# A hybrid diffusion layer: the prompt's 24 projection tiles interleaved with halves of two of the sample's tiles, in a PSUM layout of their own

## The chip, the cores and the metric

The kernel runs on one core of a Trainium2 chip. TensorE (PE) multiplies, VectorE (DVE), ScalarE (ACT) and GpSimd (POOL) compute beside it, and SyncE (SP) issues most of the transfers between the chip's memory and SBUF; TensorE writes to PSUM, of which there are 8 banks of 512 float32 columns. The metric is the device time of one execution in microseconds (us); lower is better. Each engine works through its own queue in order, and waits on semaphores for the others.

## The reference, cut to what matters

One layer is computed for two groups of tokens that share all weights: a prompt of 256 tokens and a sample of 1024 tokens, both with 1024 channels.

```python
mod = silu(c) @ w_ada + b_ada                       # six modulation vectors per group
h   = rmsnorm(x, g_norm1) * (1 + scale_m) + shift_m
proj = h @ w_in                                     # 1024 -> 3*512 + 512 + 1024 + 2*8
hc, gb, gc, z, xbc, dtf, dtb = split(proj)
out_a = gb * dwconv1d(gc * hc, w_conv_short)        # "outa"
xbc   = silu(dwconv1d(xbc, w_conv_ssd, b_conv_ssd)) # X, B, C of the scan
dt_f, dt_b = softplus(dtf + dt_bias[0]), softplus(dtb + dt_bias[1])
y   = ssd_scan(...) + reversed ssd_scan(...) + xh * d_skip
y   = rmsnorm(y * silu(z), g_ssd_norm)
x   = x + gate_m * (concat([out_a, y]) @ w_out)
...                                                 # gated ConvFFN: w_up, convolution, w_down
```

All of it is float32. The projection `h @ w_in` is the work in which the change lies, together with the cumulative sums of `dt` that the scan needs and with the modulation vectors of the FFN.

## The kernel before

**A float32 product in three.** Each operand is split into a high part (type fp32r) and the rest, and a product is made of three matmuls, hi·hi, hi·lo and lo·hi (`mm3`, L160, L162 and L164). `h` is split once. A weight tile, 128 output channels by 1024 inputs, is split when it is loaded (`wload`): a DMA brings 512 KB into a raw buffer, ACT copies it to `whi` (L151), and DVE or POOL subtracts to get `wlo` (L77; the last argument of the tile functions, `PV` or `PG`, says which). There are two buffers each of `whi` and `wlo`, and every third tile takes the single `whx`/`wlx` instead, so three split tiles can exist at a time. The raw buffers of the prompt's tiles have the tag `x` (8 of them), those of the sample's tiles the tag `raw` (2, one of which holds the sample's raw `dt` rows until `dtstage(SS)` has read them).

**Tiles of `w_in`.** Each group has 24: four each for `hc`, `gb`, `gc` and `z`, and eight for `xbc`. A tile of the prompt is 24 matmuls of 256 columns (`acc<-bc` in the rows), one of the sample 48 of 512 columns (`acc<-h`). Functions do one tile with what follows it: `xbc` (bias, convolution along the tokens; L396 is its ACT copy out of PSUM), `zproj` (copy at L409, written out by L410), and `outa` (three tiles: `hc` copied at L423, scaled at L431, `gc` multiplied into it, `gb` multiplied in, the result written out at L443 and L444 and read back by L872 for `w_out`).

**The order of the program around the change.**
1. Modulation blocks for the first norm, and beside them the sample's `xbc` tiles 0 and 1, in one loop over the inputs (L332, `N_LOOP` = 2).
2. The prompt's 24 tiles: eight `xbc`, four `zproj`, four `outa`. In between `dtstage(SP)` and `dttok(SP)`: a chain of some 20 small operations on DVE and ACT that turns the prompt's `dt` rows into decays (L458 on PE starts it; L461 to L502), and transposes of its results on PE (L513, and L523 with what L520 makes).
3. `dtstage(SS)`, the same chain for the sample; then the sample's `xbc` tiles 2 to 6, each followed by `ada(2)` to `ada(5)` in two steps: one of the four modulation vectors left, 32 small matmuls (L177) on 8 buffers `x` of `w_ada`, and transposes (L189) behind the next tile. `dttok(SS)` comes in the fifth of them, after tiles 2, 3 and 4.
4. The scan of both groups, with the sample's `z`, seventh `xbc` and `outa` tiles as fillers, and then `w_out` (L160 to L164 with `acc<-ya` and `acc<-oa`) and the FFN.

**Who sets the order.** Within this program order a list scheduler puts each engine's instructions in a row by their estimated times, and pools give out buffers: a tile with a tag waits until the buffer's last reader is done. PSUM up to `w_out` is one pool with `acc` (2 buffers of 2 banks), `yp` (1 bank) and `sa` (3 banks). When one pool is closed and another opened in its place, SBUF pools wait tile by tile (`reuse_waits="tile"`), PSUM pools for all of what the old pool held:

```python
def open_pool(name, side="left", **kw):
    if "space" not in kw:
        kw["reuse_waits"] = "tile"
```

Of the kernel before, what the change touches and what calls it, by code (L numbers as in the profile page):

```python
# [10 lines left out]
PSUM = bass.MemoryType.PSUM  # L11
DRAM = bass.MemoryType.DRAM

P = 128
# [19 lines left out]
N_LOOP = 2  # L34
# [21 lines left out]
def body(nc, tc, A):  # L56
    cnt = [0]

    def T(pool, shape, tag, bufs, dt=F32):
        cnt[0] += 1  # L60
        return pool.tile(list(shape), dt, tag=tag, bufs=bufs, name=f"{tag}_{cnt[0]}")

    def open_pool(name, side="left", **kw):
        if "space" not in kw:
            kw["reuse_waits"] = "tile"
        g = tc.tile_pool(name=name, bufs=1, side=side, **kw)
        return g, g.__enter__()

    def close_pool(g):
        g.__exit__(None, None, None)  # L70
# [8 lines left out]
    def stt(out, a, s, b, op0, op1):  # L79
        V.scalar_tensor_tensor(out=out, in0=a, scalar=s, in1=b, op0=op0, op1=op1)  # L80
# [14 lines left out]
    def smv(n):  # L95
        a, b = SMO[n]
        return sm[:, a:b]
# [25 lines left out]
    g_nrm, nrm = open_pool("nrm")  # L123
    wx = [nrm]
    g_ps, ps = open_pool("ps1", space=PSUM)

    def pacc():
        return T(ps, [P, 1024], "acc", 2)

    def pst():  # L130
        return T(ps, [P, 512], "yp", 1)
# [1 line left out]
    def psa():  # L133
        return T(ps, [P, 512], "sa", 3)
# [175 lines left out]
    for k in range(KT):  # L310
# [7 lines left out]
        x = xs[k]  # L318
# [15 lines left out]
        q, i = k // 4, k % 4  # L334
# [11 lines left out]
    for name, t0, n, v in (("p", 0, TP, 0), ("s", TP, TS, 1)):  # L346
        s = S()
# [5 lines left out]
    SP, SS = sets  # L353
# [5 lines left out]
    def proj(s, m, lo_eng):  # L359
        g = proj_halves(s, m, lo_eng)  # L360
        next(g)
        return next(g)

    def proj_halves(s, m, lo_eng):
        s.n += 1
        wh, wl = wload(A["w_in"][m], lo_eng, T(nrm, [P, KT, P], "x", 8) if s.name == "p" else None)
        pp = psa() if s.name == "p" and s.n <= 2 else pacc()
        outs = []
        for a, b in s.chunks:
            outs.append((pp[:, a:b], (lambda k, a=a, b=b: s.hi(k)[:, a:b]),  # L370
                         (lambda k, a=a, b=b: s.lo(k)[:, a:b])))
        ks = list(range(KT))
        for half in (ks[0:KT // 2], ks[KT // 2:]):
            ends = mm3(outs, wh, wl, KT, half)
            mid_mm[0] = ends[0]
            last_mm.append(ends[-1])
            yield pp[:, 0:s.T]

    def conv1d_sb(out, u, w, n):
        stt(out[:, 1:n], u[:, 0:n - 1], w[0], out[:, 1:n], ALU.mult, ALU.add)  # L380
        stt(out[:, 0:n - 1], u[:, 1:n], w[2], out[:, 0:n - 1], ALU.mult, ALU.add)

    def xbc(s, i, out, lo_eng):
        w = [smv("wcx")[:, i * 3 + t:i * 3 + t + 1] for t in range(3)]
        b = smv("bcx")[:, i:i + 1]
        if s.name == "s" and i < N_LOOP:
            u = pps[i]
            for c in range(2):
                act(out[:, c * 512:(c + 1) * 512], u[c], AF.Identity, scale=w[1], bias=b)
            stt(out[:, 1:513], u[0], w[0], out[:, 1:513], ALU.mult, ALU.add)  # L390
            stt(out[:, 513:TS], u[1][:, 0:511], w[0], out[:, 513:TS], ALU.mult, ALU.add)
            stt(out[:, 0:511], u[0][:, 1:512], w[2], out[:, 0:511], ALU.mult, ALU.add)
            stt(out[:, 511:TS - 1], u[1], w[2], out[:, 511:TS - 1], ALU.mult, ALU.add)
        else:
            pp = proj(s, 16 + i, lo_eng)
            act(out, pp, AF.Identity, scale=w[1], bias=b)  # L396
            conv1d_sb(out, pp, w, s.T)

    def zproj(s, j, lo_eng):
        for _ in zproj_halves(s, j, lo_eng):  # L400
            pass
# [45 lines left out]
    def dtcopy(s, pd):  # L447
        d4 = T(wst, [P, s.T], "raw", 2) if s.name == "s" else T(cv, [P, s.T], "cv", 4)
        for a, b in s.chunks:
            act(d4[:, a:b], pd[a // 512][:, 0:b - a], AF.Copy)  # L450
        return d4
# [53 lines left out]
    def dttok(s, v, e2, ce):  # L505
        s.tok = T(sd, [P, s.nc, 2, 40], f"tok{s.name}", 1)
        for c0 in range(0, s.nc, 4):
            cn = min(4, s.nc - c0)
            tp = psa()
            for c in range(cn):  # L510
                for i, src in enumerate((v, e2)):
                    o = (c * 2 + i) * 40
                    mm = nc.tensor.transpose(tp[:, o:o + 40], src[:, (c0 + c) * L:(c0 + c + 1) * L],  # L513
                                             ident[0:40, 0:40])
                    if c0 == c == i == 0:
                        after(mm, last_mm[-1])
            act(s.tok[:, c0:c0 + cn].rearrange("p c i r -> p (c i r)"), tp[:, 0:cn * 80], AF.Copy)
        dg = T(cv, [40, 8, 40], "cv", 4)
        for i in range(s.nc):
            V.tensor_scalar(out=dg[:, i, :], in0=ident[0:40, 0:40], scalar1=ce[:, i:i + 1],  # L520
                            scalar2=None, op0=ALU.mult)
        pdx = psa()
        nc.tensor.matmul(pdx[:, 0:s.nc * 40], ones[0:40, :],  # L523
                         dg[:, 0:s.nc].rearrange("p c r -> p (c r)"), start=True, stop=True)
        s.dec = T(sd, [P, s.nc, 40], f"dec{s.name}", 1)
        s.last_exp = act(s.dec.rearrange("p c r -> p (c r)"), pdx[:, 0:s.nc * 40], AF.Exp)
# [161 lines left out]
    PV, PG = nc.vector, nc.gpsimd  # L688
# [11 lines left out]
    for i in range(N_LOOP):  # L700
        xbc(SS, i, SS.X[i], PG)
        act(SS.X[i], SS.X[i], AF.Silu)
    for i in range(8):
        xbc(SP, i, (SP.X + bcp)[i], PG if i % 3 else PV)
        if i == 5:
            pd_p = [psa()]
            dtmm(pd_p, range(KT), lambda k: xp[k // 4][:, k % 4], TP)
            d4_p = dtcopy(SP, pd_p)
    act(xall, xall, AF.Silu)
    silu = act(bcall, bcall, AF.Silu)  # L710
    for j in range(4):
        zproj(SP, j, PG if j % 2 else PV)
        if j == 0:
            dts = dtstage(SP, d4_p, silu)
    for j in range(4):
        for _ in outa(SP, j, PG):
            pass
        if j == 0:
            dttok(SP, *dts)
    dts = dtstage(SS, d4_s, silu)  # L720


    bcs = [T(sd, [P, TS], "bc", 4) for _ in range(4)]
# [3 lines left out]
    def silu_s(i):  # L727
        after(act(xbcs[i], xbcs[i], AF.Silu), SS.last_exp)

    pend = None  # L730
    for i in range(N_LOOP, 7):
        xbc(SS, i, xbcs[i], PV)
        if pend is not None:
            next(pend)
            pend = None
        if i == 4:
            dttok(SS, *dts)
            for k in range(N_LOOP, 4):
                silu_s(k)
        if i >= 4:  # L740
            silu_s(i)
        if i < 6:
            pend = ada(i, lambda: T(nrm, [P, 1024], "x", 8))
            next(pend)
    make_aff(1, 4, "g2")
    wx[0] = None
# [116 lines left out]
    g_ps, ps = open_pool("ps2", space=PSUM)  # L863
# [382 lines left out]
```

## Time and profile before

| what | us |
|---|---|
| median of three runs | 1574.92 |
| lowest and highest of them | 1574.71 and 1576.44 |
| the profiled execution | 1575.34 |
| its span in the trace | 1573.4 |
| PE busy (8722 matmuls) | 1522.2, 97% |
| DVE, ACT and POOL busy | 1104.6, 662.1 and 514.6 |

The mean granted TensorE clock in the profiled execution was 0.993. PE is the engine to read: the time that it waits, and the time in which its clock is low, are what an order of work can save here. A row of the timeline gives the start in the span, the duration, the engine, the line, what is written and read, and in brackets how long the engine had been idle before and what it waited for; in groups, xN is the number of instructions. A row's duration on PE covers a matmul from its start to its modelled end, so matmuls in a row overlap; the step from start to start is what one costs.

### The profile page before, as it was taken

The page shows a single profiled execution, that of the slowest core. Times are in us where ns is not written, and L with a number is a line of the kernel's source. Part 1 is how long each engine was busy: PE and PEld are TensorE (multiplying, and loading weights), DVE is VectorE, ACT ScalarE, POOL GpSimd, SP SyncE. Part 2 cuts the span into 40 slices and gives each one's busy share as a digit, 9 for nine tenths or more (in the row PEclk, how much of TensorE's full clock was granted, in tenths as well). Part 3 has the DMA queues.
Part 4 walks back from the last instruction along what each step waited for, and adds up shares of the span by engine and source line. Part 5 has one row for each costly group of instructions (what it writes and reads, how often), then busy time and mean ns, then how long its engine had stood idle before and what let it go on. Part 6 is the DMA issues. An engine that isn't in the chain of part 4 may idle for free. (4 is left out here: it accounts for less than half of the span.)

```text
span 1573.4 us, 22518 instructions
## 1 busy us (share of the span) xinstructions
PE 1522.2 (97%) x8722; PEld 1296.7 (82%) x8722; DVE 1104.6 (70%) x1634; ACT 662.1 (42%) x1025; POOL 514.6 (33%) x288
## 2 busy tenths in 40 slices
PE   6989999999999999999999999999999999999997
PEld 3688667778787888888888888898888888888886
DVE  5765615367887349796666598656679878798696
ACT  6553334257777135433322253322334433433333
POOL 1445001111120001344333333333346545455452
PEclk9999999999999999999999999999999999999999
DMA  8555554343434712222222242222252333343221
GB/s 305 215 185 167 211 203 147 110 151 132 139 116 142 287 54 102 93 74 68 69 77 74 66 143 96 73 66 67 88 173 96 97 108 95 101 161 98 94 77 61
DMA packets 86908, 191.98 MB, mean 122 GB/s; under 512 B 9330, under 2 KB 36626, under 8 KB 86802
## 3 DMA queue, kind: packets, MB, share of 16 engines
q1 hardware_dynamic: 80978, 187.41, 35.1%
q10 hardware_dynamic: 5824, 3.15, 0.7%
q8 instruction: 68, 1.11, 0.3%
q14 instruction: 38, 0.31, 0.1%
HBM read 167.37 MB, written 23.15 MB: 121 GB/s over the span
## 5 line engine op out<-in xcount | busy, mean ns | idle before, releaser
L80 DVE SCALAR_TENSOR_TENSOR cc<-acc,sm,cc 128x504 f32<-128x504 f32 (+5 forms) x836 | 545.9, 665 | 110.2 <-ACT cc L986 51.9
L77 POOL TENSOR_TENSOR wlo<-raw,whi 128x1024 fp32r<-128x1024 f32 (+2 forms) x83 | 194.0, 2337 | 666.7 <-ACT whi L151 541.6
L151 ACT ACTIVATE whi<-raw 128x1024 fp32r<-128x1024 f32 x90 | 95.1, 1057 | 240.9 <-PE acc L162 218.0
L80 DVE SCALAR_TENSOR_TENSOR x<-dn,mod,x 128x288 f32<-128x288 f32 (+2 forms) x176 | 96.1, 547 | 95.1 <-PE dn L164 94.4
L77 POOL TENSOR_TENSOR dlo<-draw,dhi 128x512 fp32r<-128x512 f32 (+1 forms) x88 | 109.0, 1239 | 90.2 <-ACT dhi L1039 88.2
L160 PE MATMUL acc<-ya,whi 128*128 128x512 f32 (+1 forms) x400 | 119.4, 356 | 3.4 <-DVE cv L77 3.4
L164 PE MATMUL acc<-ya,wlo 128*128 128x512 f32 (+1 forms) x400 | 119.5, 356 | 0.0
L162 PE MATMUL acc<-ya,whi 128*128 128x512 f32 (+1 forms) x400 | 119.5, 356 | 0.0
L164 PE MATMUL acc<-oa,wlo 128*128 128x512 f32 (+1 forms) x400 | 118.9, 355 | 0.0
L162 PE MATMUL acc<-oa,whi 128*128 128x512 f32 (+1 forms) x400 | 118.7, 354 | 0.0
L160 PE MATMUL acc<-oa,whi 128*128 128x512 f32 (+1 forms) x400 | 118.2, 353 | 0.0
L160 PE MATMUL dn<-yb,dhi 128*128 128x288 f32 (+2 forms) x352 | 110.0, 313 | 5.3 <-DVE x L80 4.1
L77 POOL TENSOR_TENSOR wlx<-raw,whx 128x1024 fp32r<-128x1024 f32 (+2 forms) x32 | 74.0, 2313 | 119.2 <-ACT whx L151 104.5
L162 PE MATMUL dn<-yb,dhi 128*128 128x288 f32 (+2 forms) x352 | 109.6, 311 | 0.8 <-POOL yb L77 0.8
L164 PE MATMUL dn<-yb,dlo 128*128 128x288 f32 (+2 forms) x352 | 109.5, 311 | 0.0
L160 PE MATMUL acc<-h,whi 128*128 128x512 f32 x320 | 104.1, 404 | 0.0
L1039 ACT ACTIVATE dhi<-draw 128x512 fp32r<-128x512 f32 (+1 forms) x88 | 53.0, 602 | 121.4 <-PE dn L162 50.0
L162 PE MATMUL acc<-h,whi 128*128 128x512 f32 x320 | 101.0, 395 | 0.0
L164 PE MATMUL acc<-h,wlo 128*128 128x512 f32 x320 | 100.1, 394 | 0.0
L160 PE MATMUL dn<-g,dhi 128*128 128x288 f32 (+2 forms) x304 | 95.1, 313 | 0.0
L162 PE MATMUL dn<-g,dhi 128*128 128x288 f32 (+2 forms) x304 | 94.7, 312 | 0.3 <-POOL g L77 0.3
L164 PE MATMUL dn<-g,dlo 128*128 128x288 f32 (+2 forms) x304 | 94.7, 312 | 0.0
(340 smaller groups left out, 3631.8 us busy)
## 6 DMA issues: line engine op xcount, KB each, us to landing
raw<-in_w_up SPq DMA_DIRECT2D x88, 512.0 KB, 3.2
x<-in_w_ada SPq DMA_DIRECT2D x32, 512.0 KB, 5.4
draw<-in_w_down SPq DMA_DIRECT2D x64, 256.0 KB, 2.7
x<-in_w_in SPq DMA_DIRECT2D x24, 512.0 KB, 3.3
raw<-in_w_in SPq DMA_DIRECT2D x22, 512.0 KB, 4.3
xs<-in_w_ad SPq DMA_DIRECT2D x16, 512.0 KB, 8.4
csb<-csds SPq DMA_DIRECT2D x16, 512.0 KB, 3.9
raw<-in_w_out SPq DMA_DIRECT2D x16, 512.0 KB, 3.2
```

Of the source, the lines that this page charges most:

```text
L77: (eng or V).tensor_tensor(out=out, in0=a, in1=b, op=op)
L80: V.scalar_tensor_tensor(out=out, in0=a, scalar=s, in1=b, op0=op0, op1=op1)
L151: act(hi, raw, AF.Copy)
L160: nc.tensor.matmul(o, wh[:, k, :], rh(k), start=k == 0, stop=False)
L162: nc.tensor.matmul(o, wh[:, k, :], rl(k), start=False, stop=False)
L164: mm = nc.tensor.matmul(o, wl[:, k, :], rh(k), start=False, stop=k == n - 1)
L1039: act(wh, raw, AF.Copy)
```

## The change

The prompt's part (stage 2) gets a PSUM layout of its own. The first pool is closed after the loop of stage 1. A second has `pj` (three buffers of one bank) for the prompt's tiles, `sa` as before, and a single `acc` of two banks; a third, opened after `dtstage(SS)`, has the layout of before. PSUM pools now also wait tile by tile, here and at `w_out`.

In the prompt's part two of the sample's tiles are done, each in two halves of four inputs (`xbc_halves`): tile 2 after the prompt's `xbc` 3 and 7, tile 3 after the last `zproj` and after the second `outa`. The split weights of such a tile stay in their buffers from the first half to the second. `ada(2)` follows the second `outa` and is finished after the third; the first step of `ada(3)` follows the fourth. The loop of stage 3 begins with tile 4, so that one tile of the sample instead of three lies between `dtstage(SS)` and `dttok(SS)`.

```diff
     def open_pool(name, side="left", **kw):
-        if "space" not in kw:
+        if kw.get("space") != DRAM:
             kw["reuse_waits"] = "tile"
...
     def pacc():
-        return T(ps, [P, 1024], "acc", 2)
+        return T(ps, [P, 1024], "acc", 1 if ph_p[0] else 2)
+    ph_p = [False]
+    def pj():
+        return T(ps, [P, 512], "pj", 3)
...
-        pp = psa() if s.name == "p" and s.n <= 2 else pacc()
+        pp = pj() if s.name == "p" else pacc()
...
     def xbc(s, i, out, lo_eng):
+        for _ in xbc_halves(s, i, out, lo_eng):
+            pass
+    def xbc_halves(s, i, out, lo_eng):
...
-            pp = proj(s, 16 + i, lo_eng)
+            g = proj_halves(s, 16 + i, lo_eng)
+            next(g)
+            yield
+            pp = next(g)
             act(out, pp, AF.Identity, scale=w[1], bias=b)
             conv1d_sb(out, pp, w, s.T)
+            yield
...
+    close_pool(g_ps)
+    g_ps, ps = open_pool("ps2", space=PSUM)
+    ph_p[0] = True
+    def ada_s(cc):
+        return ada(cc, lambda: T(nrm, [P, 1024], "x", 8))
+    xs_g = [xbc_halves(SS, i, SS.X[i], PV) for i in (2, 3)]
     for i in range(8):
         xbc(SP, i, (SP.X + bcp)[i], PG if i % 3 else PV)
...
+        if i in (3, 7):
+            next(xs_g[0])
...
     for j in range(4):
         zproj(SP, j, PG if j % 2 else PV)
         if j == 0:
             dts = dtstage(SP, d4_p, silu)
+    next(xs_g[1])
     for j in range(4):
         for _ in outa(SP, j, PG):
             pass
         if j == 0:
             dttok(SP, *dts)
+        if j == 1:
+            next(xs_g[1])
+            pend = ada_s(2)
+            next(pend)
+        if j == 2:
+            next(pend)
+    pend = ada_s(3)
+    next(pend)
     dts = dtstage(SS, d4_s, silu)
+    close_pool(g_ps)
+    g_ps, ps = open_pool("ps3", space=PSUM)
+    ph_p[0] = False
...
-    for i in range(N_LOOP, 7):
+    for i in range(4, 7):
         xbc(SS, i, xbcs[i], PV)
         if pend is not None:
             next(pend)
...
         if i == 4:
             dttok(SS, *dts)
             for k in range(N_LOOP, 4):
                 silu_s(k)
-        if i >= 4:
-            silu_s(i)
+        silu_s(i)
         if i < 6:
-            pend = ada(i, lambda: T(nrm, [P, 1024], "x", 8))
+            pend = ada_s(i)
             next(pend)
```

Lines below the first edit move down by 5, 13 or more: L160, L162 and L164 become L165, L167 and L169; L177 becomes L182, L396 L408, L409 L422, L458 L471, L493 L506, L513 L526, and L523 L536. Three places show how instructions stand. The names end in a running number; `pj_...` and `acc_...` are PSUM accumulators, `whi_...`, `whx_...` and so on split weights, `x_...` raw buffers.

ACT at the prompt's last `z` tiles, before. L472 and L493 belong to `dtstage(SP)`, and each L409 frees the accumulator of a `z` tile.

```order
L472 ACTIVATE cv_160_912<-cv_161_914 40x256 [waits DVE_49,Activation_49]
L409 ACTIVATE xl_172_1004<-acc_171_979 128x256 [waits DMAHW5_49,PE_49]
L151 ACTIVATE whi_184_1076<-x_183_1074 128x1024
L410 DMA zd_114_565<-xl_172_1004 128x2x128 [waits DMAHW0_49,Activation_49]
L151 ACTIVATE whi_189_1112<-x_188_1110 128x1024 [waits DMAHW7_49,PE_49,Pool_49]
L493 ACTIVATE cv_157_904<-cv_157_904 40x256 [waits DVE_49]
L409 ACTIVATE xl_177_1038<-acc_176_1013 128x256 [waits DMAHW6_49,PE_49]
```

The same place with the change:

```order
L485 ACTIVATE cv_164_974<-cv_165_976 40x256 [waits DVE_49,Activation_49]
L156 ACTIVATE whi_187_1136<-x_186_1134 128x1024 [waits DMAHW6_49,PE_49]
L422 ACTIVATE xl_176_1066<-pj_175_1041 128x256 [waits DMAHW5_49,PE_49]
L423 DMA zd_114_565<-xl_176_1066 128x2x128 [waits DMAHW1_49,Activation_49]
L506 ACTIVATE cv_161_966<-cv_161_966 40x256 [waits DVE_49]
L156 ACTIVATE whx_192_1169<-x_191_1167 128x1024 [waits PE_49,Pool_49]
L515 ACTIVATE cv_163_971<-cv_163_971 40x256 [waits DVE_49]
L422 ACTIVATE xl_181_1100<-pj_180_1075 128x256 [waits DMAHW7_49,PE_49]
```

The last `z` tile's accumulator still comes free behind L506 (L493 before) and now behind two more instructions; but `pj` has three buffers, and PE has the first half of the sample's tile 3 ahead of the tile that takes that buffer again.

SP before, at the loads of the prompt's last two `outa` tiles (`x<-in_w_in`) and the first of `ada(2)` (`x<-in_w_ada`):

```order
L149 DMA x_231_1376<-in_w_in 128x1024 [waits DMAHW6_49,DMAHW1_49,Pool_49]
L490 DMA csdp_109_560<-cv_161_914 4x2x128 [waits DMAHW3_49,DVE_49]
L490 DMA csdp_109_560<-cv_161_914 4x2x128 [waits DMAHW4_49]
L490 DMA csdp_109_560<-cv_161_914 4x2x128 [waits DMAHW5_49,DVE_49]
L490 DMA csdp_109_560<-cv_161_914 4x2x128 [waits DMAHW6_49]
L149 DMA x_236_1409<-in_w_in 128x1024 [waits DMAHW7_49,Pool_49]
L149 DMA x_241_1445<-in_w_in 128x1024 [waits DMAHW0_49,Pool_49]
L174 DMA x_264_1585<-in_w_ada 128x1024 [waits DMAHW1_49,Pool_49]
```

SP with the change, where the last loads of `ada(2)` and the first for the third `outa` stand:

```order
L179 DMA x_232_1410<-in_w_ada 128x1024 [waits DMAHW6_49,Pool_49]
L456 DMA oad_113_564<-xl_221_1356 128x256 [waits DMAHW7_49,Activation_49]
L457 DMA oad_113_564<-xl_222_1358 128x256 [waits DMAHW0_49,DVE_49]
L154 DMA x_235_1427<-in_w_in 128x1024 [waits DMAHW1_49,PE_49]
L154 DMA x_240_1460<-in_w_in 128x1024 [waits DMAHW2_49,PE_49]
L154 DMA x_245_1496<-in_w_in 128x1024 [waits DMAHW6_49,DMAHW3_49,PE_49]
```

And PE with the change, from the middle of the first step of `ada(2)` to the first `outa` tile behind it:

```order
L182 MATMUL sa_224_1390<-x_226_1392,sc_7_77 32x512
L182 MATMUL sa_224_1390<-x_225_1391,sc_7_77 32x512
L182 MATMUL sa_223_1389<-x_232_1410,sc_7_77 32x512 [waits DMAHW6_49]
L182 MATMUL sa_223_1389<-x_231_1409,sc_7_77 32x512 [waits DMAHW5_49]
L182 MATMUL sa_223_1389<-x_230_1408,sc_7_77 32x512 [waits DMAHW2_49]
L182 MATMUL sa_223_1389<-x_229_1407,sc_7_77 32x512 [waits DMAHW1_49]
L182 MATMUL sa_224_1390<-x_232_1410,sc_7_77 32x512
L182 MATMUL sa_224_1390<-x_231_1409,sc_7_77 32x512
L182 MATMUL sa_224_1390<-x_230_1408,sc_7_77 32x512
L182 MATMUL sa_224_1390<-x_229_1407,sc_7_77 32x512
L165 MATMUL pj_238_1433<-bc_36_173,whi_236_1429 128x256 [waits Activation_49]
L167 MATMUL pj_238_1433<-bc_38_175,whi_236_1429 128x256
```

Before, the loads of the `outa` tiles waited for POOL, the last reader of an earlier prompt tile, and those of `ada(2)` came behind them. Now the eight buffers `x` are with `ada(2)` when the third `outa` asks for three, and the load of `x_235_1427` waits for PE, for the row of L182 that reads `x_226_1392` last (the first of the rows above); the weights made of it, `whi_236_1429`, are what the tile `pj_238_1433` reads.

PE at `dttok(SS)`, before: `acc_277_1627` and `acc_295_1737` are the sample's tiles 3 and 4, with `acc_261_1531`, tile 2, ahead of them. L458 starts `dtstage(SS)` ahead of all three.

```order
L458 MATMUL sa_248_1484<-raw_117_568,cst_2_66 40x512
L458 MATMUL sa_249_1487<-raw_117_568,cst_2_66 40x512 [waits PE_49]
L160 MATMUL acc_261_1531<-h_52_225,whx_259_1527 128x512 [waits DVE_49]
...
L164 MATMUL acc_295_1737<-h_107_532,wlo_294_1734 128x512 x2
L189 MATMUL sa_296_1789<-cst_2_66,x_290_1727 128x128 [waits DVE_49,Activation_49]
L189 MATMUL sa_296_1789<-cst_2_66,x_290_1727 128x128 x3
L189 MATMUL sa_297_1796<-cst_2_66,x_291_1729 128x128 [waits Activation_49]
L189 MATMUL sa_297_1796<-cst_2_66,x_291_1729 128x128 x3
L513 MATMUL sa_299_1804<-cst_2_66,cv_247_1483 128x40 [waits PE_49]
```

With the change (`acc_295_1745` is tile 4, `acc_319_1892` tile 5):

```order
L471 MATMUL sa_282_1694<-raw_117_568,cst_2_66 40x512 [waits DVE_49]
L471 MATMUL sa_283_1697<-raw_117_568,cst_2_66 40x512 [waits Activation_49]
L165 MATMUL acc_295_1745<-h_52_225,whi_293_1741 128x512 [waits DVE_49]
...
L169 MATMUL acc_295_1745<-h_107_532,wlo_294_1742 128x512 x2
L194 MATMUL sa_296_1797<-cst_2_66,x_279_1689 128x128 x4
...
L165 MATMUL acc_319_1892<-h_78_362,whx_317_1888 128x512 x2
L526 MATMUL sa_299_1812<-cst_2_66,cv_281_1693 128x40 [waits DVE_49,PE_49]
L167 MATMUL acc_319_1892<-h_79_365,whx_317_1888 128x512 x2
```

Between the start of the chain (L458, now L471) and the first instruction that needs its end (L513, now L526) stood three tiles of the sample; now there are one tile and 20 matmuls of the next.

More of the change, by code (lines that the diff above doesn't have):

```diff
@@ L728, in silu_s @@
         after(act(xbcs[i], xbcs[i], AF.Silu), SS.last_exp)
-    pend = None
-    for i in range(N_LOOP, 7):
+    for i in range(4, 7):
         xbc(SS, i, xbcs[i], PV)
```

## The prediction

> **What bounds the kernel now.** I read the page's first part, then PE's waits, then the stretch of the prompt's tiles by windows and the timeline, and last the place where the PSUM pool changes at `w_out`.
>
> ```profile
> PE 1522.2 (97%) x8722; PEld 1296.7 (82%) x8722; DVE 1104.6 (70%) x1634; ACT 662.1 (42%) x1025; POOL 514.6 (33%) x288
> ```
>
> PE is busy for all but 51 us of the span, and the change neither adds nor removes a matmul. So it can only move the idle time and the clock of PE. PE's waits, in all, times, longest:
>
> ```profile
> PE yp L243 <- DVE cv L77: 11.0, 1, 11.0
> ...
> PE acc L160 <- DVE cv L77: 3.4, 1, 3.4
> ...
> PE sa L523 <- DVE cv L520: 3.4, 1, 3.4
> ...
> PE acc L160 <- ACT xl L409: 3.3, 1, 3.3
> ...
> PE acc L160 <- ACT bcp L396: 1.0, 1, 1.0
> ```
>
> The 11.0 us are the start of the kernel, untouched. The other four are where the change works: the first at `w_out`, the rest in the prompt's part. There the windows show busy time by engine, then the clock:
>
> ```profile
> core 0: us, PE busy (x) PEld busy (x) DVE busy (x) ACT busy (x) POOL busy (x), PEclk, DMA share, GB/s
> 110.00:120.00 10.00, 6.67 (x51) 6.47 (x50) 8.28 (x14) 3.05 (x6) 4.99 (x2) 0.93 0.44 145
> 120.00:130.00 10.00, 6.58 (x43) 6.21 (x43) 6.32 (x7) 3.58 (x8) 7.11 (x3) 0.84 0.40 137
> 130.00:140.00 10.00, 10.00 (x77) 10.00 (x76) 2.37 (x2) 3.36 (x5) 4.70 (x2) 0.89 0.42 124
> ```
>
> and PE's rows show that an idle of 3.3 or 3.4 us costs twice:
>
> ```profile
> 113.71 0.28 PE L162 MATMUL acc<-bc,whx 128*128 128x256 f32 x1
> 113.83 0.28 PE L164 MATMUL acc<-bc,wlx 128*128 128x256 f32 x1
> 117.44 0.39 PE L160 MATMUL acc<-bc,whi 128*128 128x256 f32 x1 [3.33 <-ACT xl L409]
> ...
> 118.61 0.41 PE L160 MATMUL acc<-bc,whi 128*128 128x256 f32 x1
> 118.81 0.42 PE L162 MATMUL acc<-bc,whi 128*128 128x256 f32 x1
> ...
> 121.81 0.38 PE L160 MATMUL acc<-bc,whi 128*128 128x256 f32 x1
> ...
> 128.74 0.58 PE L523 MATMUL sa<-cv,ones 40*128 40x80 f32 x2 [3.42 <-DVE cv L520]
> ```
>
> A prompt matmul steps by 0.12 us (113.71 to 113.83), but 15 of them, from 118.61 to 121.81, take 3.2 us, 0.213 each: 15 × 0.093 = 1.4 us lost to the clock. The idle ahead of 128.74 is followed by as much: the window from 130 has PE at 10.00 busy with a clock of 0.89, 11% of 10 us or 1.1, and some of it falls before 130; I take 1.4 again. The part now loses 1.0 + 3.3 + 3.4 + 2.8 = 10.5 us.
>
> The reason for the 3.3 us: ACT frees the accumulator, and stood in `dtstage(SP)`.
>
> ```profile
> 116.71 0.42 ACT L493 ACTIVATE cv<-cv 40x256 f32<-40x256 f32 x1 [4.44 <-DVE cv L492]
> 117.03 0.36 ACT L409 ACTIVATE xl<-acc 128x256 f32<-128x256 f32 x1
> ```
>
> **What goes.** L409 (now L422) still stands behind that chain, but the tile that takes the bank again is now the third behind it, with a half of a sample tile ahead. Half a tile is 12 pairs of 512 columns at 0.46 us, 5.5 us, and two tiles of the prompt are 2 × 24 × 0.12 = 5.8:
>
> ```profile
> 168.24 0.62 PE L160 MATMUL acc<-h,whx 128*128 128x512 f32 x2
> 168.70 0.62 PE L162 MATMUL acc<-h,whx 128*128 128x512 f32 x2
> ```
>
> 11.3 us of cover for an evacuation that was 3.3 late: that wait and its 1.4 of clock go. The 1.0 behind the `xbc` tiles goes with the third bank. Without this cover they would come back in full, 4.7 us. Two steps cost nothing: SP passes the `ada` loads ahead of the last `outa` loads, and the first `ada` loads go out while PE runs tiles whose weights are in already; the added PSUM pools issue no instruction, and the wait at their border is for tiles that were read some tiles ago.
>
> **What comes.** Prices of the steps of a weight tile, and of what stands between them:
>
> ```profile
> 102.91 2.40 POOL L77 TENSOR_TENSOR wlo<-x,whi 128x1024 fp32r<-128x1024 f32 x1 [3.34 <-ACT whi L151]
> 92.01 1.06 ACT L151 ACTIVATE whi<-x 128x1024 fp32r<-128x1024 f32 x1 [2.06 <-PE acc L162]
> 78.54 2.01 ACT L702 ACTIVATE xs<-xs 128x1024 f32<-128x1024 f32 x2
> 80.45 0.55 ACT L396 ACTIVATE xp<-sa,sm 128x256 f32<-128x256 f32 x1
> 79.23 1.22 DVE L77 TENSOR_TENSOR wlx<-x,whx 128x1024 fp32r<-128x1024 f32 x1
> 87.80 0.99 DVE L80 SCALAR_TENSOR_TENSOR xp<-acc,sm,xp 128x255 f32<-128x255 f32 x2
> 81.11 0.28 PE L160 MATMUL acc<-bc,whx 128*128 128x256 f32 x1
> 169.72 3.64 PE L177 MATMUL sa<-x,sc 128*32 128x512 f32 x32
> ```
>
> 1. *The fourth prompt tile.* The first three now share three banks, and the first bank's evacuation stands behind the two silus of the sample's tiles on ACT and `wlx` on DVE. PE gets there at 81.1, as before, since the same work is ahead. The silus end at 80.5, `whx` at 81.5, `wlx` on DVE at 82.7, the two convolution steps at 83.7: 2.5 us late by these rows. The silus wait for the loop's last matmuls, which now have no prompt rows between them and come a little sooner; I take 1.8, ends 1.0 and 2.6.
> 2. *Three sets of weights.* The sample's tile keeps its set between its halves, so two are left for the prompt, and a tile's set is the one that the tile before it has just left. From its release it takes 1.06 + 2.40, and 0.1 to 0.3 of passing on: 3.6 to 3.75 us. PE has other work, counted in its row of instructions, of 2.1 us at the eighth `xbc` tile, 3.1 at the third tile of `outa` 0 and 2.5 at that of `outa` 1. Waits of 1.5, 0.5 and 1.2; ends 0.8 and 2.0 for the first, 0 and 1.8 for the others.
> 3. *`dttok(SP)`*: L536 (L523 before) waits for the same two DVE steps behind the same convolution. PE comes later by what terms 1 and 2 cost, which the chain partly shares. I take 2.0 of the 3.4; ends 1.0 and 3.4.
> 4. *The third `outa`.* The load of its first weights now waits for the 14th of the 32 matmuls of `ada(2)`: 14/32 × 3.64 = 1.6 us into them. Then DMA, ACT and POOL follow one another, and PE has nothing in its row but the rest of `ada(2)` and two matmuls. The loads, from issue to landing:
>
> ```profile
> x<-in_w_in SPq DMA_DIRECT2D x24, 512.0 KB, 3.3
> x<-in_w_ada SPq DMA_DIRECT2D x32, 512.0 KB, 5.4
> ```
>
> 1.6 + 3.3 + 1.1 + 2.4 + 0.2 of passing on = 8.6, against 3.64 + 0.24 = 3.9 of PE: a wait of about 4.8. If the transfer takes 5.4, as in the bursts of `ada`, it is 6.9; with one at 2.0 us, 3.5. I take 3.3, as it is the first of its burst. Behind it POOL's 2.4 per tile keeps up with PE's 2.9.
> 5. *`dttok(SS)`.* The sample's chain, from its first ACT step to its last product on DVE:
>
> ```profile
> 160.50 1.24 ACT L461 ACTIVATE cv<-sa,rows 40x512 f32<-40x512 f32 x2
> ...
> 180.99 1.20 DVE L77 TENSOR_TENSOR cv<-cv,cv 40x1024 f32<-40x1024 f32 x1
> ```
>
> 182.2 − 160.5 = 21.7 us, of which two weight steps of DVE in its middle, 2 × 1.2, now stand elsewhere: 19.3. Before, three tiles of 11 us and two steps of `ada` covered it. Now one tile (11.0), eight transposes (an estimate of 1.0) and 20 matmuls (4.6) do, 16.6 us: a wait of 2.7, and 0.3 for the later ones of the same chain, 3.0; ends 1.5 and 5.
> 6. *The clock.* Waits 4 and 5 are as long as those that cost 1.4 us each: one surely, the other as likely as not to be long enough in one piece, 1.4 + 1.0 = 2.4; ends 1.4 and 3.5.
>
> The Trainium skill ("TensorE: Matmul & The Clock Gate", Part 1, "What's actually happening") states that the array's clock is halved after an idle window of about 3.4 us, stays so for about as long a busy one, and that the window runs free. The 3.2 us of slow steps behind an idle of 3.33 agree. By that rule wait 5 costs either nothing or a full window, an estimate of 0 or 1.7 us, which would make the sum 1579.1 or 1580.8. It speaks against turning several short waits into one long one.
>
> Together 1.8 + 3.2 + 2.0 + 4.8 + 3.0 + 2.4 = 17.2 us, against 10.5: +6.7.
>
> **At `w_out`** the first accumulator waits for all of the old pool, the last `outa` tile's DVE step among it, and the clock falls.
>
> ```profile
> 508.32 1.22 DVE L77 TENSOR_TENSOR cv<-acc,cv 128x1024 f32<-128x1024 f32 x1
> 509.69 0.59 PE L160 MATMUL acc<-ya,whi 128*128 128x256 f32 x2 [3.39 <-DVE cv L77]
> ...
> 515.51 0.51 PE L160 MATMUL acc<-oa,whi 128*128 128x256 f32 x2
> 515.86 0.51 PE L162 MATMUL acc<-oa,whi 128*128 128x256 f32 x2
> ...
> 522.21 0.51 PE L162 MATMUL acc<-oa,whi 128*128 128x256 f32 x2
> 513.86 3.14 SPq L872 DMA_DIRECT2D oa<-oad  x2
> oa<-oad SPq DMA_DIRECT2D x2, 384.0 KB, 3.7
> ```
>
> Tile by tile it takes the banks of the tile before the last and could start at 506.3: 3.4 us and the clock's 1.6 sooner (a pair steps by 0.35 us, so that the 12 pairs before 515.51 are worth 4.2; they took 5.8), 5.0 in all. But two loads that it reads late, `oa`, are issued at 513.9 and 516.7 whatever PE does, since they follow the last `outa` tile out to memory and back. They land at 517.6 and 520.4. Row 522.21 needs the second; now it can run at 520.4. So 1.8 of the 5.0 is left, ends 0 and 5.0. Late next is the second `oa` load, instead of DVE.
>
> **The sum.** +6.7 − 1.8 = +4.9, on 1575.3 for the profiled execution (0.4 above the median): 1580 us.
>
> **The rivals.**
> - *The halves do cover the preparation (faster).* ACT, DVE and POOL would be a tile or more ahead behind each 5.5 us half, so that terms 1, 2 and 4 vanish with one clock loss: 1.8 + 3.2 + 4.8 + 1.4 = 11.2 off, 1569. It turns on one thing, whether a weight set and a buffer `x` come free 3.5 us (for `x`, 7 us) ahead of use. For it speaks POOL's 3.34 us of idle ahead of 102.91: it had time. Against it, these waits are for buffers, not for engines.
> - *`w_out` pays in full (no change).* If `oa` is not what PE waits for, because its transfers land sooner or PE arrives later there, 3.2 us more come back: 1577. The rows of SP speak against it.
> - *The transfers are slower (slower still).* SP sends six loads in one burst after `ada(2)`; at 5.4 us the first costs 2.1 more, and if the second and third are as late with it, two waits of some 2 us follow: 1586. DMA at 0.40 to 0.44 busy there speaks against it.
>
> **How the numbers follow.** The measurement can tell 0.2%, 3.1 us, from no change: 1571.8 to 1578.1 counts as the same. My forecast, 1576.5 to 1583.5 by its own ends, has a chance of 0.50, of which 0.07 lies below 1578.1. The first rival has 0.2, the second 0.18, the third 0.12. Faster 0.2; same 0.18 + 0.07 = 0.25; slower 0.43 + 0.12 = 0.55. Leaving out a tenth on each side, the range goes into the first rival and to the third: 1570 to 1586.
>
> **What would show it.** Right: L422 of the last `z` tile ends no wait of PE; a wait of 4 to 5 us of PE at an `outa` tile behind L182, for POOL or ACT, with steps of 0.21 us behind it; one of 2 to 4 us at L526 or L536 late in the stretch, for DVE or ACT; waits of 0.5 to 2 us for `wlo` at prompt tiles; at `w_out` no wait for DVE, but 1 to 3 us for `oa`. Wrong: no wait behind L182, so that the buffer came free in time; no wait at L526, so that the chain is shorter than 16.6 us beside less DVE work; or a new wait in the scan, whose orders I took as unchanged.

## The result and the profile after

The changed kernel took 1581.5 us, the median of 6 runs (1581.19 to 1585.21), against 1575.89 for the kernel before in 6 runs beside it: a ratio of 1.0039, with a 95% interval of 1.0024 to 1.0053. It is slower by about 0.4%. Its profiled execution took 1581.34 us, with a span of 1579.3 and a mean clock of 0.990.

The waits for `xl` (L409, now L422), for `bcp` and for DVE at `w_out` are gone, and the one at L523 (now L536) is down from 3.4 to 0.8. PE's waits in the prompt's part and at `dttok(SS)` in the changed kernel's timeline, each row with its place:

```profile
83.58 0.36 PE L165 MATMUL pj<-bc,whx 128*128 128x256 f32 x1 [1.74 <-DVE xp L80]
105.58 0.39 PE L169 MATMUL pj<-bc,wlo 128*128 128x256 f32 x1 [1.24 <-POOL wlo L77]
136.49 0.39 PE L169 MATMUL pj<-bc,wlo 128*128 128x256 f32 x1 [0.43 <-POOL wlo L77]
140.60 0.45 PE L536 MATMUL sa<-cv,ones 40*128 40x80 f32 x2 [0.84 <-DVE cv L533]
149.38 0.39 PE L169 MATMUL pj<-bc,wlo 128*128 128x256 f32 x1 [1.02 <-POOL wlo L77]
163.62 0.39 PE L165 MATMUL pj<-bc,whi 128*128 128x256 f32 x1 [3.11 <-ACT whi L156]
166.04 0.58 PE L169 MATMUL pj<-bc,wlo 128*128 128x256 f32 x1 [1.92 <-POOL wlo L77]
212.66 0.30 PE L526 MATMUL sa<-cst,cv 40*128 40x40 f32 x1 [2.98 <-DVE cv L77]
```

They add up to 13.3 us. The clock behind the last three is in the windows (behind the window's length stands PE's busy time; the clock is third from the end):

```profile
160.00:170.00 10.00, 4.97 (x28) 4.26 (x21) 0.82 (x1) 4.16 (x5) 6.36 (x3) 0.73 0.95 351
170.00:180.00 10.00, 10.00 (x81) 10.00 (x80) 4.62 (x6) 4.27 (x6) 7.27 (x4) 0.93 0.66 197
210.00:220.00 10.00, 7.34 (x37) 5.27 (x41) 8.90 (x21) 1.94 (x4) 0.00 (x0) 0.83 0.31 91
```

Where the time stands can be read from rows that both kernels have. The sums of the scan that wait for `xd` (called the row of the scan below) come at 268.64 before and at 276.38 after, 7.7 us later, of which 0.7 were lost ahead of the fourth prompt tile: it could have started at 83.58 − 1.74 = 81.84, and did at 81.11 before.

```profile
268.64 0.66 PE L535 MATMUL sa<-cst,xs 128*128 128x128 f32 x4 [1.26 <-DVE xd L77]
522.91 0.39 PE L160 MATMUL acc<-ya,whi 128*128 128x512 f32 x1
```

```profile
276.38 0.66 PE L548 MATMUL sa<-cst,xs 128*128 128x128 f32 x4 [1.26 <-DVE xd L77]
526.43 1.01 PE L165 MATMUL acc<-oa,whi 128*128 128x256 f32 x2 [2.71 <-DMA oa<-oad]
529.94 0.39 PE L165 MATMUL acc<-ya,whi 128*128 128x512 f32 x1
```

Those are rows of before, then of after. From the first to the last row of each there are 254.27 and 253.56 us: `w_out` gave back 0.7. So the prompt's part from there on and `dttok(SS)` cost 7.0, `w_out` gains 0.7, and at 530 us the changed kernel is 7.0 late; its span is 5.9 longer. The rest of the difference is in the main the clock in the FFN: an idle of 2.74 us, which both kernels have (it ends at 988.54 before and at 995.55 after), was followed by a lower clock in the trace of before and by none in that of after.

```profile
990.00:1000.00 10.00, 10.00 (x51) 8.75 (x50) 4.57 (x8) 1.43 (x2) 3.00 (x2) 0.88 0.13 41
```

```profile
985.00:1000.00 15.00, 12.26 (x75) 11.14 (x74) 11.34 (x19) 4.31 (x7) 4.76 (x3) 1.00 0.35 110
```

The first window is of before (clock 0.88), the second of after (1.00). Nothing of the change is there. The twelve matmuls behind this idle took 4.09 us before and 2.53 after; over the eleven traces of this case they took 4.1 to 4.6 in six and 2.5 in five. So a single trace carries an uncertainty of 1.5 to 2 us from this one place.

### The profile page after: what moved, and what is told of

It is laid out like the page before. It is cut to its first block, busy times and chain, and to the rows that moved or that the text cites. A ratio compares the mean times of both kernels' runs of the same rounds, so it can differ in the third digit from the quotient of the medians.

```text
span 1579.3 us, 22515 instructions
## 1 busy us (share of the span) xinstructions
PE 1523.7 (96%) x8722; PEld 1296.8 (82%) x8722; DVE 1098.6 (70%) x1634; ACT 662.8 (42%) x1025; POOL 514.9 (33%) x288
## 5 line engine op out<-in xcount | busy, mean ns | idle before, releaser
L156 ACT ACTIVATE whi<-raw 128x1024 fp32r<-128x1024 f32 x91 | 96.2, 1057 | 236.7 <-PE acc L167 210.1
L165 PE MATMUL acc<-oa,whi 128*128 128x512 f32 (+1 forms) x400 | 118.8, 355 | 2.7 <-DMA oa<-oad 2.7
L167 PE MATMUL acc<-ya,whi 128*128 128x512 f32 (+1 forms) x400 | 119.3, 356 | 0.0
L165 PE MATMUL acc<-ya,whi 128*128 128x512 f32 (+1 forms) x400 | 119.2, 355 | 0.0
L169 PE MATMUL acc<-ya,wlo 128*128 128x512 f32 (+1 forms) x400 | 119.1, 355 | 0.0
L167 PE MATMUL acc<-oa,whi 128*128 128x512 f32 (+1 forms) x400 | 119.0, 355 | 0.0
L169 PE MATMUL acc<-oa,wlo 128*128 128x512 f32 (+1 forms) x400 | 119.0, 355 | 0.0
L165 PE MATMUL dn<-yb,dhi 128*128 128x288 f32 (+2 forms) x352 | 109.4, 311 | 5.3 <-DVE x L80 4.1
L167 PE MATMUL dn<-yb,dhi 128*128 128x288 f32 (+2 forms) x352 | 109.0, 310 | 0.8 <-POOL yb L77 0.8
L165 PE MATMUL acc<-h,whi 128*128 128x512 f32 x336 | 109.5, 404 | 0.0
L169 PE MATMUL dn<-yb,dlo 128*128 128x288 f32 (+2 forms) x352 | 108.9, 309 | 0.0
L167 PE MATMUL acc<-h,whi 128*128 128x512 f32 x336 | 106.3, 396 | 0.0
L169 PE MATMUL acc<-h,wlo 128*128 128x512 f32 x336 | 105.4, 395 | 0.0
L167 PE MATMUL dn<-g,dhi 128*128 128x288 f32 (+2 forms) x304 | 94.8, 312 | 0.3 <-POOL g L77 0.3
L165 PE MATMUL dn<-g,dhi 128*128 128x288 f32 (+2 forms) x304 | 95.1, 313 | 0.0
L169 PE MATMUL dn<-g,dlo 128*128 128x288 f32 (+2 forms) x304 | 94.8, 312 | 0.0
```

The source lines that it names most:

```text
L156: act(hi, raw, AF.Copy)
L165: nc.tensor.matmul(o, wh[:, k, :], rh(k), start=k == 0, stop=False)
L167: nc.tensor.matmul(o, wh[:, k, :], rl(k), start=False, stop=False)
L169: mm = nc.tensor.matmul(o, wl[:, k, :], rh(k), start=False, stop=k == n - 1)
```

## The experiments

My theory after the result: the loss is made of places in queues and of buffers, above all of `ada(2)` holding the eight buffers `x` ahead of the third `outa`, and of the missing cover at `dttok(SS)`; the tile-by-tile PSUM waits bring almost nothing at `w_out`. The rival: these places are where work is short (POOL, DVE), so that each order only moves the waits. For each experiment the median of its runs stands with the ratio to the kernel before and its 95% interval.

**The PSUM waits alone, on the kernel before.**

```diff
-        if "space" not in kw:
+        if kw.get("space") != DRAM:
             kw["reuse_waits"] = "tile"
```

> The kernel before, with the PSUM pools waiting tile by tile, and nothing else of the change. My theory: PE starts w_out 3.4 us sooner and at full clock, but then waits about 2.7 us for the last oa loads, as in the changed kernel, so that between 0 and 2 us are left: 1573 to 1575 us, no more than 0.1%. The rival, that this edit pays in full and hides what the rest costs: 5 us, 1570 us, and no wait for oa.

Measured: 1575.28 us, ratio 0.9993 (0.9981 to 1.0005). The wait for DVE at `w_out` goes, and one for the `oa` loads comes:

```profile
518.34 1.01 PE L160 MATMUL acc<-oa,whi 128*128 128x256 f32 x2 [2.75 <-DMA oa<-oad]
```

So this edit by itself gives nothing that can be measured, as the theory has it: a transfer that follows the last `outa` tile out and back was hidden behind the PSUM wait.

**The PSUM waits undone, in the changed kernel** (the same edit backwards).

> The changed kernel with PSUM pools that wait for all of the old pool, as before, at all three borders. My theory: tile by tile is what makes the two new borders free. The prompt's first tile then waits for the last convolution step of the loop's tiles, about 6.5 us with 1.5 us of clock behind it, in place of the 1.7 us at the fourth; the sample's tile 4 waits for the copies of dtstage(SS), 3 to 4 us, in place of the 3.0 at dttok(SS); w_out starts behind DVE again, 0.7 us worse: 1581.3 + 8.0 - 1.7 + 0.7 + 0.7 = 1589 us, 1585 to 1592. The rival, that the borders hide under other work: 0.7 us, 1582.

Measured, one run: 1585.43 us, with these rows at the first border, at the second, and at `w_out`:

```profile
78.32 0.55 PE L165 MATMUL pj<-bc,whx 128*128 128x256 f32 x1 [6.09 <-DVE xs L80]
...
199.26 0.73 PE L165 MATMUL acc<-h,whi 128*128 128x512 f32 x2 [0.77 <-ACT cv L474]
...
520.53 0.62 PE L165 MATMUL acc<-ya,whi 128*128 128x256 f32 x2 [3.38 <-DVE cv L77]
```

The first border costs 6.1 us, close to the 6.5; the second only 0.8 instead of 3 to 4, as the copies of `dtstage(SS)` are done sooner than I took them to be. The new layout depends on waits tile by tile: without them the row of the scan comes at 280.36 in place of 276.38, 4.0 later. The one time on record says less, since it lies only 0.2 us above the slowest run of the changed kernel.

**`ada(2)` and `ada(3)` out of the prompt's part.**

```diff
-            pend = ada_s(2)
-            next(pend)
-        if j == 2:
-            next(pend)
-    pend = ada_s(3)
-    next(pend)
     dts = dtstage(SS, d4_s, silu)
...
+    pend = ada_s(2)
+    next(pend)
     for i in range(4, 7):
...
-        if i < 6:
-            pend = ada_s(i)
-            next(pend)
+        pend = ada_s(i - 1)
+        next(pend)
+    next(pend)
```

> The changed kernel with ada(2) and ada(3) taken out of the prompt's part; ada(2) to ada(5) stand behind dtstage(SS) and the sample's tiles 4, 5 and 6. My theory: the eight buffers x are then free for the third outa, the 5.0 us of waiting there and 2.2 us of clock behind it go, while the wait at dttok(SS) stays at 3 to 4 us since ada(2) before tile 4 adds PE work but the transposes now come 18 matmuls sooner: 1581.3 - 7.2 + 0.5 = 1574.6 us, 1573 to 1576. The rival, that the wait at the third outa comes from POOL's pace or from the sets of weights: it stays, and the time is 1580 to 1582.

Measured: 1576.18 us, ratio 1.0006 (0.9996 to 1.0016). Both waits at the third `outa` are gone; the dt chain is waited for twice:

```profile
196.46 0.65 PE L526 MATMUL sa<-cst,cv 40*128 40x40 f32 x2 [4.53 <-DVE cv L77]
258.39 0.66 PE L548 MATMUL sa<-cst,xs 128*128 128x128 f32 x4 [3.09 <-DVE xd L77]
```

The time is just above what I expected. By the medians some 5 us of the change's 6, and by the row of the scan (272.10 in place of 276.38) 4.3 of the 7.7, are therefore in where the two `ada` steps stand. The 3.1 us at the start of the scan I had not expected.

**Half of `ada(2)` left out**, so that four buffers `x` stay free.

```diff
-        for k0 in (0, 4):
+        for k0 in ((0,) if cc == 2 else (0, 4)):
...
-                                     ws[q][:, i * 512:(i + 1) * 512], start=k0 == 0, stop=k0 == 4,
+                                     ws[q][:, i * 512:(i + 1) * 512], start=k0 == 0, stop=k0 == 4 or cc == 2,
```

> The changed kernel with the second half of the inputs of ada(2) left out: its modulation vector is then wrong, PE has 16 matmuls less (1.8 us) and four of the eight buffers x stay free. My theory: the loads for the third outa start early, and 5.0 us of waiting and 2.2 us of clock go beside the 1.8: 1581.3 - 9.0 = 1572.3 us, 1571 to 1574. The rival, that buffers x are not what the load waits for: 1.8 less, 1579.5 us, and the wait of 3 us for ACT and 2 us for POOL at the third outa stays.

Measured: 1580.83 us, ratio 1.0038 (1.0026 to 1.0051): 8.5 us above what I expected, and nearer to the rival's 1579.5. The waits are still there, 1.74 and 1.93 us, together 1.4 less than in the changed kernel. The row of the scan comes 1.8 us sooner (274.61), no more than the 16 matmuls left out are worth; the low clock behind L526, longer here, took part of the rest. SP's and ACT's rows tell why the waits stay:

```profile
153.38 0.97 SPq L457 DMA_DIRECT2D oad<-xl  x1
154.45 5.77 SPq L154 DMA_DIRECT2D x<-in_w_in  x6
158.60 0.60 ACT L188 ACTIVATE x<-sa 128x512 f32<-128x512 f32 x1 [0.26 <-PE sa L182]
159.09 1.05 ACT L156 ACTIVATE whi<-x 128x1024 fp32r<-128x1024 f32 x1
```

In the changed kernel the six loads are issued at 158.84, as soon as `ada(2)` gives up the buffers. Here they are issued at 154.45, directly behind the store L457 of the second `outa`, which waited for DVE; and when they have landed, `whi` (L156) stands on ACT behind the copies L188 of the very `ada(2)`. In the rows, the buffer was the last of three things in a row to be late, and taking it away uncovered the other two.

**`dttok(SS)` behind tile 5.**

```diff
-        if i == 4:
+        if i == 5:
             dttok(SS, *dts)
-            for k in range(N_LOOP, 4):
+            for k in range(N_LOOP, 5):
                 silu_s(k)
-        silu_s(i)
+        if i >= 5:
+            silu_s(i)
```

> The changed kernel with dttok(SS) behind the sample's tile 5 instead of tile 4. My theory: the chain of dtstage(SS) is 20 us long, and with two tiles ahead PE doesn't wait for it: 3.0 us of wait and 1.3 us of clock go, 1581.3 - 4.3 = 1577.0 us, 1576 to 1578.5. The rival, that the scan behind needs the result as soon as it can be had, so that the wait only moves: 1580 to 1582.

Measured: 1583.84 us, ratio 1.0047 (1.0030 to 1.0065), not faster than the changed kernel. The wait at L526 went and another of the same length came, at the matmuls of `ada(4)`:

```profile
215.19 1.42 PE L182 MATMUL sa<-x,sc 128*32 128x512 f32 x8 [2.79 <-DVE mod L198]
```

and DVE's rows show L198, which frees the bank `sa` for them, behind the chain:

```profile
211.22 1.20 DVE L77 TENSOR_TENSOR cv<-cv,cv 40x1024 f32<-40x1024 f32 x1
...
213.83 1.21 DVE L77 TENSOR_TENSOR cv<-cv,ces 40x1024 f32<-40x1024 f32 x1
214.96 0.27 DVE L198 TENSOR_REDUCE mod<-sa 128x8 f32<-128x32 f32 x2
```

With the reader of the result moved away, PE waits as long for another instruction that stands behind the same chain on DVE. Here the rival is right.

**The sample's tiles done whole.**

```diff
-        if i in (3, 7):
+        if i == 3:
             next(xs_g[0])
+            next(xs_g[0])
...
     next(xs_g[1])
+    next(xs_g[1])
...
-            next(xs_g[1])
             pend = ada_s(2)
```

> The changed kernel with the sample's tiles 2 and 3 done whole, after the prompt's fourth xbc and after the last z, so that no set of weights is held between halves; ada stays where the change puts it. Theory on the sets: the three waits for wlo (1.2, 0.4 and 1.0 us) go. By the traces so far I expect more: ada(2) then follows the second outa directly, 5.5 us sooner, and its last loads, which land near 154 us, are late by 3 to 5 us; the third outa waits as before. 1581.3 - 2.7 + 4 = 1582.6 us, 1580 to 1585. The rival, that the sets are all that ties these tiles: 1578.6 us and no wait of PE for loads of ada.

Measured, one run: 1580.71 us. The three waits for `wlo` between 105 and 150 us are gone, so they did come from the set of weights that a half keeps. No load of `ada(2)` was late, against my expectation; L536 took the gain instead, and the row of the scan stands at 277.81, 1.4 us later than in the changed kernel:

```profile
143.79 2.35 DVE L533 TENSOR_SCALAR cv<-cst,cep 40x40 f32<-40x40 f32 x2
146.28 0.42 PE L536 MATMUL sa<-cv,ones 40*128 40x80 f32 x2 [3.58 <-DVE cv L533]
```

**A version from the findings, in two forms.** The first has one tile of the sample in two halves behind the last `z`, `ada(2)` between them, and tile 3 back in the loop.

```diff
-        pp = pj() if s.name == "p" else pacc()
+        pp = (psa() if s.n <= 2 else pj()) if s.name == "p" else pacc()
...
-        if i in (3, 7):
-            next(xs_g[0])
...
-    next(xs_g[1])
+    xs_g = xbc_halves(SS, 2, SS.X[2], PV)
+    next(xs_g)
+    pend = ada_s(2)
+    next(pend)
+    next(xs_g)
     for j in range(4):
...
         if j == 0:
             dttok(SP, *dts)
+            next(pend)
+            pend = None
-        if j == 1:
-            next(xs_g[1])
-            pend = ada_s(2)
-            next(pend)
-        if j == 2:
-            next(pend)
-    pend = ada_s(3)
-    next(pend)
...
-    for i in range(4, 7):
+    for i in range(3, 7):
...
-        silu_s(i)
+        if i >= 4:
+            silu_s(i)
```

> A version built from the findings: the change's PSUM layout and waits, the first two prompt tiles in sa as before; one tile of the sample, tile 2, in two halves right behind the last z, with the first step of ada(2) between them and its second step after the first outa; tile 3 back in the loop, ada(3) to ada(5) behind tiles 3, 4 and 5, dttok(SS) behind tile 4. My theory: the half tile behind ada(2) (5.5 us) covers the loads for outa, no set is shared, and two tiles cover dtstage(SS), so that of the 10.5 us that the kernel before loses in the prompt's part 1 to 2 are left and w_out gains 0.5: 1575.3 - 9 - 0.5 = 1566 us, 1563 to 1569. The rival, that every order only moves the waits (to DVE's queue, as when dttok was put later, or to SP's): 1573 to 1577.

Measured: 1573.93 us, ratio 0.9993 (0.9984 to 1.0002), where the rival had it. Two waits had taken the place of the old ones:

```profile
137.19 0.68 PE L536 MATMUL sa<-cv,ones 40*128 40x80 f32 x2 [3.92 <-DVE cv L533]
171.51 0.73 PE L165 MATMUL acc<-h,whi 128*128 128x512 f32 x2 [3.01 <-ACT cv L474]
```

DVE's rows at the first of them:

```profile
110.50 0.16 DVE L511 COPY cep<-cv 8x2 f32<-8x2 f32 x1
...
131.48 5.14 DVE L80 SCALAR_TENSOR_TENSOR cv<-cv,sm,cv 128x255 f32<-128x255 f32 x2 [0.93 <-ACT cv L444]
136.66 0.39 DVE L533 TENSOR_SCALAR cv<-cst,cep 40x40 f32<-40x40 f32 x2
```

L533 reads only `cep`, ready at 110.7, and stands 26 us later behind the convolution of the first `outa`, which takes 5.1 us beside POOL. The second wait is the border to the third PSUM layout: with the first prompt tiles in `sa`, tile 3 now falls on banks that ACT's copies of `dtstage(SS)` (L474) still read. A third wait is an old one: at `w_out` PE waits 3.39 us for DVE (506.62), as in the kernel before, although the pools wait tile by tile. Why it waits so here, and not in the changed kernel, is not shown.

The first two are orders of two lines:

```diff
     next(xs_g)
+    dttok(SP, *dts)
     for j in range(4):
...
         if j == 0:
-            dttok(SP, *dts)
             next(pend)
...
-    dts = dtstage(SS, d4_s, silu)
     close_pool(g_ps)
     g_ps, ps = open_pool("ps3", space=PSUM)
     ph_p[0] = False
+    dts = dtstage(SS, d4_s, silu)
```

> The version with one tile in halves behind the last z, with two edits: dttok(SP) stands ahead of the first outa instead of behind it, so that DVE makes its diagonal (L533) ahead of the convolution of outa; and the third PSUM layout is opened ahead of dtstage(SS) instead of behind it, so that its copies don't hold banks that the sample's tile 3 takes. My theory: both waits were places in a queue or in PSUM, not work; the 3.9 us at L536 and the 3.0 us at tile 3 go, with about 2.5 us of clock, and less than 1 us comes at the border: 1573.9 - 8.5 = 1565.5 us, 1563 to 1569, about 0.6% faster than the kernel before. The rival, that DVE's or ACT's work is what is short there: the waits come back within 10 us of the same place, 1572 to 1575.

Measured: 1565.17 us, ratio 0.9933 (0.9920 to 0.9946). That is what I expected; it beats the kernel before by 0.7% and, by the two ratios, the changed one by about 1%. L533 now follows L511 (111.94) at once, and at `w_out` the wait is again one for `oa`, 2.82 us:

```profile
112.14 0.39 DVE L533 TENSOR_SCALAR cv<-cst,cep 40x40 f32<-40x40 f32 x2
```

Where PE had idled, its windows (busy behind the length, clock third from the end) are full:

```profile
110.00:120.00 10.00, 10.00 (x64) 6.03 (x63) 3.10 (x10) 1.82 (x4) 0.00 (x0) 1.00 0.28 87
120.00:130.00 10.00, 10.00 (x61) 8.63 (x62) 2.56 (x2) 5.83 (x8) 6.46 (x3) 1.00 0.95 362
130.00:140.00 10.00, 10.00 (x86) 10.00 (x86) 6.02 (x9) 4.76 (x8) 8.06 (x4) 1.00 0.47 161
```

**One of its edits on the kernel before:** `dttok(SP)` ahead of the first `outa`, nothing else.

> The kernel before with dttok(SP) ahead of the first outa, and nothing of the change. My theory: the 3.4 us of PE at L523 and the 1.4 us of clock behind them were a place in DVE's queue, behind the convolution of the first outa; the chain itself is done at 117.6 us. They go, while the 3.3 us at the last z stay: 1575.3 - 4.8 = 1570.5 us, 1569 to 1572.5. The rival, that the chain is late: PE waits as long, only earlier, 1574 to 1576.

Measured: 1574.11 us, ratio 0.9988 (0.9979 to 0.9997), a gain of 2 us (0.5 to 3.3 by the interval) instead of 4.8. Both old waits, 3.33 and 3.42 us, are gone, and one of 5.50 stands there:

```profile
119.69 0.33 PE L513 MATMUL sa<-cst,cv 40*128 40x40 f32 x1 [5.50 <-DVE cv L77]
```

Without half a tile ahead of it, PE is there before the chain: this time the chain is late. The place in the queue and the cover are needed together, and the version above has both.

## Why the prediction was right

The forecast of 1580 us, slower, with 0.55 on slower, met 1581.5. The direction and the places of the waits came as told; that the time agrees to 1.5 us is in part luck. By rows the changed kernel is 7.0 us late at 530 us, against 4.9 forecast: 0.7 lost ahead of the fourth tile, 0.6 more at a wait of the scan (L551 at 246.61: 1.67, where L538 waited 1.03 before) and 1.1 less gained at `w_out` were not in the sum, while the terms that it priced in the prompt's part and at `dttok(SS)` came to 16.9 of the 17.2. The clock in the FFN, which no step spoke of, gave 1.6 of it back in these two traces. By its steps:

- *What goes.* As told: no wait for `xl` or `bcp` is left.
- *The fourth prompt tile:* 1.8 forecast, 1.74 measured. Its start, 83.7 by the rows of before, came at 83.58; but PE got there 0.7 later than the prediction took, so the tile as a whole is 2.5 late.
- *Three sets of weights:* 1.5, 0.5 and 1.2 forecast, 1.24, 0.43 and 1.02 measured. The whole tiles showed that the held set is the cause.
- *`dttok(SP)`:* 2.0 forecast, 0.84 measured, just under its lower end of 1.0. The step named the right two DVE operations and the right queue, but laid the price on how late PE comes. By the rows PE came 0.5 later against the convolution than before (139.76 − 137.28 = 2.48, and 125.32 − 123.38 = 1.94); what fell was the time of the two operations themselves, 0.39 in place of 2.35. Before, and with the whole tiles (143.79), a subtraction of POOL ran beside them (126.06 to 128.41, and 143.45 to 145.95); here POOL was idle (139.32 to 140.51). With 2.35 the wait would have been 0.84 + 1.96 = 2.8, an estimate. That it is a place on DVE's queue, and not the chain, the last version showed. The rows are of before and of after:

```profile
126.24 2.35 DVE L520 TENSOR_SCALAR cv<-cst,cep 40x40 f32<-40x40 f32 x2
...
140.16 0.39 DVE L533 TENSOR_SCALAR cv<-cst,cep 40x40 f32<-40x40 f32 x2
```
- *The third `outa`:* 4.8 forecast, 3.11 + 1.92 = 5.03 measured. The sum was right for the changed kernel. The load was issued at 158.84, ACT took it up at 162.51 and POOL at 163.64, as told. Its account of the cause was too short, since it named the buffer alone; with half of `ada(2)` left out SP's and ACT's queues were nearly as late.
- *`dttok(SS)`:* 3.0 forecast, 2.98 measured. Its cause, a chain of 19 us against 16.6 of cover, is as told (20.2 measured, from ACT's L474 at 192.29 to the end of DVE's product at 212.51), but moving the reader did not help, which the prediction did not see: L198 stands behind the same chain.
- *The clock:* 2.4 forecast. Behind the third `outa`, 23 matmuls step by 0.21 us (rows below), 2.1 us more than at full clock; behind L526 the four pairs from 212.89 take 3.3 us in place of 1.8, 1.4 more: 3.6 in all, half as much again as forecast: 0.7 because the first stretch of low clock lasted 4.9 us and not the 3.2 seen before, and 0.4 because the second, taken as likely as not, came. The Trainium skill ("TensorE: Matmul & The Clock Gate", Part 1, "What's actually happening") has the clock come down after an idle window of about 3.4 us that runs free; here idles of 2.98 and 2.71 us brought it down and one of 2.74 did so in one trace and not in the other, which agrees with a window that runs free but not with 3.4 us as a least length of one idle.

```profile
166.42 0.41 PE L165 MATMUL pj<-bc,whi 128*128 128x256 f32 x1
166.63 0.41 PE L167 MATMUL pj<-bc,whi 128*128 128x256 f32 x1
...
171.33 0.34 PE L169 MATMUL pj<-bc,wlx 128*128 128x256 f32 x1
...
212.89 1.22 PE L167 MATMUL acc<-h,whx 128*128 128x512 f32 x2
213.91 1.05 PE L169 MATMUL acc<-h,wlx 128*128 128x512 f32 x2
...
216.17 0.63 PE L169 MATMUL acc<-h,wlx 128*128 128x512 f32 x2
```

- *`w_out`:* 1.8 forecast, 0.7 measured. The wait moved to the `oa` loads, as told, but to the first of the two and not the second: the row at 526.43 (L165, hi by hi) reads the one issued at 521.58, which took the longer of the two landings, 4.8 us, and not the 3.7 of the prediction. And the clock fell behind these 2.7 us as it had behind the old wait: from 526.43 to 529.94 3.51 us pass for what took 1.86 before (521.05 to 522.91). The prediction counted the clock's 1.6 as saved.

Of the rivals, the first (the halves cover the preparation) falls: with the halves where the change puts them the waits for weights came as forecast. It comes true in another order, at 1565 us. The second falls with the PSUM edit alone (nothing gained), and the third with the six loads, which landed 4.0 us after their issue in the median: the first tile's wait is 5.0, and none came for the loads of the second and the third.

## What to carry to other kernels

Price an insertion by the buffers that it takes (weight sets, load buffers, banks) and by what it moves ahead of others in each in-order queue, not by the engine time that it fills: here the waits that came stood at such places, and the low clock behind three of them. When a wait is taken away, look at what stands next in the same queue, since an instruction whose inputs were ready 26 us ago may be late only because of what is written ahead of it. Work that is to cover a chain must stand between the chain's start and its reader, and the reader ahead of the next work on the chain's engine.

## What the runs showed of the hardware

The same two steps of `outa`'s convolution on DVE took 1.00 us in the changed kernel where POOL was idle, 2.85 where a subtraction of POOL ran beside them (136.92 to 139.32), and 5.14 in the first version (row above), where POOL had two in a row (up to 133.66, and 134.00 to 136.34). The two small operations of L533 (L520) took 0.39 and 2.35 in the same way, which moved a wait of PE by 2 us.

```profile
137.28 2.85 DVE L80 SCALAR_TENSOR_TENSOR cv<-cv,sm,cv 128x255 f32<-128x255 f32 x2 [0.92 <-ACT cv L444]
149.23 1.00 DVE L80 SCALAR_TENSOR_TENSOR cv<-cv,sm,cv 128x255 f32<-128x255 f32 x2 [0.58 <-ACT cv L444]
```

And the clock fell behind idles of PE as short as 1.81 us, and not behind each longer one. With `dttok(SS)` behind tile 5 the window from 420 to 425 us, behind an idle of 1.81, has a clock of 0.66, and so has the changed kernel's, behind one of 2.03. With `ada(2)` and `ada(3)` moved an idle of 3.09 at 258.39 was followed by a clock of 1.00. The wait of 3.39 at `w_out` cost 1.6 us of clock in the kernel before and none in the last experiment, where `w_out` is the same (508.19; the window from 510 to 515 has 1.00). The runs of one kernel spread by 4 to 9 us; how much of that is the clock is not shown.
